# The feed-forward behind all blocks, in two halves of 1024 tokens, with seven quarter products in place of eight

## The chip, the cores and the metric

The kernel runs on one core of one Trainium2 chip. The metric is the time of one execution on the device, in microseconds (us); less is better. Inside the core five engines work side by side, each on its own instruction queue and in the order of that queue: TensorE (PE in the profile; its weight loads are PEld), VectorE (DVE), ScalarE (ACT), GpSimd (POOL) and SyncE (SP), which here issues all transfers (DMAs) between DRAM and the on-chip memory SBUF. TensorE adds its products up in the banks of PSUM, from where VectorE or ScalarE read them.

## What is computed

One layer of a hybrid decoder, for one prompt of 2048 tokens (width 1024) and for 64 sample rows (8 sequences of 8 tokens). Shapes and what doesn't matter here are left out:

```python
def hybrid_layer(x, c, ...):
    sh1, sc1, gt1, sh2, sc2, gt2 = split(silu(c) @ w_ada + b_ada, 6)
    h = rms_norm(x, norm1_g) * (1 + sc1) + sh1
    q, k, v, g, u, gate_r, gate_s = split(h @ w_in)
    ret = rms_normalize(retention(rotary(q), rotary(k), v)) * silu(g)
    ssm = gelu(s5(u)); ssm = ssm * sigmoid(ssm @ w_glu)
    merged = sigmoid(gate_r) * (ret @ w_br) + sigmoid(gate_s) * (ssm @ w_bs)
    x = x + gt1 * (merged @ w_out)
    h2 = rms_norm(x, norm2_g) * (1 + sc2) + sh2
    ff = square(relu(h2 @ w_up)) @ w_down        # 1024 -> 4096 -> 1024
    return x + gt2 * ff, ...
y = rms_norm(hybrid_layer(x, c, ...), norm_f_g)
```

The change concerns h2, ff and what follows. All is float32.

## The kernel before, in words

**Products.** A float32 operand is split in two parts: the high one (a copy rounded to the type fp32r, made by ScalarE) and the low one (the rest, a subtraction on GpSimd or VectorE). Each product is made as three matmuls, high by high, high by low and low by high, added up in PSUM. The unit is a matmul of a 128x128 stationary tile with 128x512 moving columns.

**Weights.** `plan` (L155) lays out one stream of weight tiles of 128x2x512 (512 KB). `fetch` (L162, its DMA on L165) loads a tile into one of four raw buffers, `refill` (L169) splits it: high half on L175, low half on L177, into a ring of five. One tile is fetched and split for each one used, so a load is issued as soon as the low half of an old tile is done.

**Blocks.** The tokens go through the layer in four blocks of 512; the sample's 64 rows ride along with block 1 (two more matmuls for each 128 rows of a weight, `sample_products`, L215). `super_block` (L1136) calls `block` (L191) for each group of 512 output columns, in the order u, q, k, v, g, gates, glu, br, bs, wo0, wo1, and then the feed-forward loop (L1434): up0, then for g from 1 to 7 up{g} followed by dn{g-1} in two halves a and b, and at the end dn7a with both halves. Each up group takes 96 matmuls and each dn half 48, so a block's feed-forward takes 16 x 96. What evacuates the banks: `ev_up` (L1385: ScalarE's relu, VectorE's product with the bank, ScalarE's and GpSimd's split of the result) and `ev_dn` (L1406: VectorE multiplies by gt2, L1411, and adds to the row tile x1, L1412). The activations and x1 stay in SBUF.

**Side work.** Everything that isn't a dense product (norms, retention, the S5 recurrence, outputs) is written as generators that `spawn` queues and `tick` advances a step after each piece of products. So the second norm (`norm_t`, L353 to L380: scale, eight transposes on TensorE at L365, eight modulations on VectorE at L377, split) is spawned by the evacuation of wo1 row tile by row tile, the first norm of the next block (`ln1`, L1094) at up7, and `output` (L1459: final norm, store) by dn7a. A scheduler then orders each engine's instructions; buffers come from pools, each name from a pool of fixed size, and a new tile waits until the readers of the buffer's old one are done. The pools that matter are `units` (15 buffers of 1 MB), `w2` (six tiles of up to 128x512) and `w4` (two of up to 128x1024); a tile that `work` gives comes from w2 or w4 by its size alone.

## Time and profile before

| what | value |
|---|---|
| times of three runs | 3221.25, 3223.88, 3227.47 us |
| median | 3223.88 us |
| span of the profiled execution | 3214.3 us |
| difference of the median to that span | 9.6 us |
| TensorE busy | 3066.6 us, 14460 matmuls |
| VectorE, GpSimd, ScalarE busy | 1782.5, 1527.6, 985.9 us |
| read from DRAM, written | 345.55 MB, 28.79 MB |

The span is the time from the first to the last instruction of one profiled execution. In rows of groups, `out<-in` are the kernel's tile names, then partitions x elements and type of both sides, `xN` the count, then busy time, mean time of one in ns, and the idle time of the engine just before them with what ended it. Rows of one tile or line give min/median/max in ns. Rows of the chain of waits give the start, the time it took in the chain, and what it was; rows of a timeline start, duration, engine, line; rows of stretches the length, then busy time (and count) of PE, PEld, DVE, ACT and POOL, the granted TensorE clock, the busy share of the DMA engines, and GB/s.

### The profile page before, as it was taken

How to read it: one execution, taken by the hardware profiler on the slowest of the kernel's cores; microseconds unless marked ns; L12 is line 12 of the kernel's file. 1: busy time of each engine (PE TensorE's matmuls, PEld its weight loads, DVE VectorE, ACT ScalarE, POOL GpSimd, SP SyncE). 2: the span in 40 equal slices, each digit the busy share in tenths (PEclk: the TensorE clock that was granted, in tenths of full speed). 3: DMA queues.
4: the chain of work that ended last, by engine and by line, in shares of the span. 5: the costliest groups of instructions: out<-in, count | busy, mean ns of one | idle time of the engine just before them, and what ended most of it. 6: DMA issues, size and time to landing. Idle time of an engine off the chain costs nothing.

```text
span 3214.3 us, 37740 instructions
## 1 busy us (share of the span) xinstructions
PE 3066.6 (95%) x14460; PEld 2524.0 (79%) x14460; DVE 1782.5 (55%) x3177; ACT 985.9 (31%) x1430; POOL 1527.6 (48%) x724
## 2 busy tenths in 40 slices
PE   7889999999899999899999899999998899999998
PEld 3667788888688887788887688888887788888886
DVE  5978445444867154645458673354547663354545
ACT  2323434222322232332324123332333223333332
POOL 2442465555343534354543334645563433646653
PEclk9989999999999999999999899999999999999999
DMA  8474542323464423132223642422323652333331
GB/s 221 154 237 144 165 138 79 100 97 98 117 185 119 115 71 118 59 99 79 80 85 100 185 150 74 126 98 98 98 95 103 189 152 81 119 100 97 98 99 66
DMA packets 233400, 376.80 MB, mean 117 GB/s; under 512 B 67766, under 2 KB 78534, under 8 KB 229115
## 3 DMA queue, kind: packets, MB, share of 16 engines
q1 hardware_dynamic: 233220, 374.40, 37.7%
q8 instruction: 113, 1.85, 0.2%
q14 instruction: 67, 0.55, 0.0%
HBM read 345.55 MB, written 28.79 MB: 116 GB/s over the span
## 4 chain that ended last, share of the span: by engine, by line
PE 75%; DVE 17%; DMA 3%; issue 2%; SPq 1%; POOL 0%; ACT 0%; DVEq 0%; ACTq 0%; POOLq 0%
PE pd_up L212 20%; PE pd_gs L212 5%; PE pd_gr L212 5%; PE pd_wo L212 5%; PE pd_br L212 3%; PE pd_g L212 2%; PE pd_bs L212 2%; DVE m L377 2%; PE pd_v L212 2%; PE pd_dn4a L212 1%; PE pd_dn3a L212 1%; PE pd_dn1a L212 1%; PE pd_dn5a L212 1%; PE pd_dn2a L212 1%; PE pd_dn0a L212 1%
## 5 line engine op out<-in xcount | busy, mean ns | idle before, releaser
L177 POOL TENSOR_TENSOR wlo<-wraw,whi 128x1024 fp32r<-128x1024 f32 x472 | 1189.6, 2525 | 1388.5 <-ACT whi L175 1169.7
L175 ACT ACTIVATE whi<-wraw 128x1024 fp32r<-128x1024 f32 x504 | 531.0, 1059 | 1403.5 <-PE pd_up L212 271.9
L212 PE MATMUL pd_up<-h2l,whi 128*128 128x512 f32 (+1 forms) x1152 | 422.8, 368 | 6.0 <-DVE h2l L380 3.3
L212 PE MATMUL pd_up<-h2h,whi 128*128 128x512 f32 (+1 forms) x1152 | 419.6, 368 | 8.6 <-ACT h2h L379 7.6
L212 PE MATMUL pd_up<-h2h,wlo 128*128 128x512 f32 (+1 forms) x1152 | 417.2, 367 | 0.0
L1389 DVE TENSOR_TENSOR tv<-tu,pd_up 128x512 f32<-128x512 f32 x128 | 87.8, 688 | 513.7 <-ACT tu L1388 513.0
L1412 DVE TENSOR_TENSOR x<-x,td 128x512 f32<-128x512 f32 x256 | 339.3, 1325 | 7.5
L212 PEld LDWEIGHTS pd_up<-h2h,whi 128*128 128x128 f32 x1152 | 217.2, 190 | 46.2 <-ACT h2h L379 9.3
L212 PEld LDWEIGHTS pd_up<-h2l,whi 128*128 128x128 f32 x1152 | 219.0, 190 | 43.0 <-DVE h2l L380 8.1
L212 PEld LDWEIGHTS pd_up<-h2h,wlo 128*128 128x128 f32 x1152 | 218.5, 190 | 34.9
L1391 POOL TENSOR_TENSOR al<-tv,ah 128x512 fp32r<-128x512 f32 x128 | 177.3, 1395 | 35.7 <-ACT ah L1390 32.8
L212 PE MATMUL pd_gr<-hh,whi 128*128 128x512 f32 x256 | 103.4, 405 | 2.3 <-DVE gU L1220 2.3
L212 PE MATMUL pd_gs<-hl,whi 128*128 128x512 f32 x256 | 101.0, 394 | 0.0
L212 PE MATMUL pd_gr<-hl,whi 128*128 128x512 f32 x256 | 101.0, 394 | 0.0
L212 PE MATMUL pd_gs<-hh,whi 128*128 128x512 f32 x256 | 100.7, 395 | 0.0
L212 PE MATMUL pd_wo<-whi,mh 128*128 128x512 f32 x256 | 100.3, 393 | 0.0
L212 PE MATMUL pd_wo<-wlo,mh 128*128 128x512 f32 x256 | 100.3, 393 | 0.0
L212 PE MATMUL pd_wo<-whi,ml 128*128 128x512 f32 x256 | 99.8, 394 | 0.0
L212 PE MATMUL pd_gs<-hh,wlo 128*128 128x512 f32 x256 | 99.4, 395 | 0.0
L212 PE MATMUL pd_gr<-hh,wlo 128*128 128x512 f32 x256 | 99.2, 393 | 0.0
L377 DVE TENSOR_SCALAR m<-pt,s,modT 128x128 f32<-128x128 f32 x256 | 85.6, 403 | 8.6 <-PE pt L365 6.8
L1388 ACT ACTIVATE tu<-pd_up 128x512 f32<-128x512 f32 x128 | 76.0, 595 | 45.0 <-PE pd_up L212 43.9
(674 smaller groups left out, 6897.9 us busy)
## 6 DMA issues: line engine op xcount, KB each, us to landing
wraw<-in_w_in_dram SPq DMA_DIRECT2D x144, 512.0 KB
wraw<-in_w_up_dram SPq DMA_DIRECT2D x128, 512.0 KB
wraw<-in_w_down_dram SPq DMA_DIRECT2D x128, 512.0 KB
s5p<-s5c SPq DMA_DIRECT2D x32, 1024.0 KB
wraw<-in_w_ada_dram SPq DMA_DIRECT2D x32, 512.0 KB
wraw<-in_w_out_dram SPq DMA_DIRECT2D x32, 512.0 KB
x<-in_x_prompt_dram SPq DMA_DIRECT2D x20, 512.0 KB
wa<-in_w_ada_dram SPq DMA_DIRECT2D x8, 1024.0 KB
```

The costliest lines, as they stand in the source:

```text
L175: a = nc.scalar.activation(hi, raw, AF.Copy)
L177: l = eng.tensor_sub(lo, raw, hi)
L212: nc.tensor.matmul(banks[j][:, cols], a, b, start=(k == 0 and z == 0), stop=(k == nk - 1 and z == 2))
L377: nc.vector.tensor_scalar(m[:, a], pt[:, a], s[:, k:k + 1], b[:, k:k + 1], op0=ALU.mult, op1=ALU.add)
L1388: nc.scalar.activation(t, p, AF.Relu)
L1389: V.tensor_mul(t2, t, p)
L1391: nc.gpsimd.tensor_sub(act[g][1][:, j], t2, act[g][0][:, j])
L1412: V.tensor_add(x[:, e], x[:, e], t)
```

## The change

The feed-forward leaves the blocks. A block ends with wo1. The row tile x1 is stored to DRAM (`x1d`), and `norm_quarters` replaces the second norm: the same scale, transposes and modulations, but the normed activations are written to DRAM (`s2d`) as seven "parts" of 128x2048 float32 (1 MB each; for blocks 1 and 3 the sums and differences with the parts of the block before, which are read back). Behind block 3, `feed_forward` runs two halves of 1024 tokens. Its products are made by Strassen's scheme in the variant of Winograd: the weight's and the activations' quarters are combined by sums and differences so that seven quarter products do the work of eight.

A half consists of five macros: one "up" of 16 quads (256 columns of w_up each) and four "down" (each 1024 rows of w_down) of four quads. A quad has seven products p in the order 1, 5, 6, 3, 7, 2, 4, each of four 128-rows x three matmuls: 84 matmuls, in four PSUM banks a (1, 6, 7), d (5, 3), b (2), c (4), which are read out after each product, also between products that add to one bank. For each quad two loads of 512 KB bring the weights (`quad_fetch`), and for each product `quad_split` makes the weight's quarter, for p = 5, 6, 7, 4 by a difference on GpSimd, and splits it (ScalarE; low half on VectorE for 7, 2, 4 and on GpSimd otherwise). At each macro's start all seven parts of the activations are loaded (`part_load`, two halves of 512 KB into w4 each) and split (`part_split`) into 14 tiles that the whole macro uses; the part for p is loaded within the last quad of the macro before, and a new part's split waits for the old part's last product. `evac_up` combines the up products with relu and square into seven parts again and stores them (`sd`, 2 DMAs a quad). `evac_down` adds each product, scaled by gt2, into an accumulator of 1024 tokens by 256 columns. After the last down macro's quads, `turn_back` transposes the accumulator (16 transposes a quad), adds x1 (loaded into w4), and after the fourth applies the final norm in place (32 instructions of 128x256, norm_f_g in w4) and stores (32 DMAs).

The sample's feed-forward becomes "side" tiles of the old stream, drawn one after each unit of the other products: its up in block 2, its down in block 3. `units` has 17 buffers in place of 15, the pool of small tiles 10 in place of 12, the block orders "h" and "jd" go, and the first norm of the next block is spawned before wo0. The pools of the blocks and those of the feed-forward take turns in the same memory. The core of the diff:

```diff
+ORDER = (1, 5, 6, 3, 7, 2, 4)
+BANK = {1: "a", 6: "a", 7: "a", 5: "d", 3: "d", 2: "b", 4: "c"}
...
+    def part_load(self, macro, p):
+        kind, k, c = macro
+        src = (self.s2d[k] if kind == "up" else self.sd[k][c])[PART[p]]
+        ts = []
+        for h in range(2):
+            t = self.work("sw", [P, 2, 512])
+            self.nc.sync.dma_start(t.rearrange("p a n -> p (a n)"), src[:, 1024 * h:1024 * h + 1024])
+            ts.append(t)
+        return ts
+
+    def part_split(self, p, ts):
+        hi = self.sring.tile([P, 4, 512], F32R, tag="s", name="shi")
+        lo = self.sring.tile([P, 4, 512], F32R, tag="s", name="slo")
+        for h, t in enumerate(ts):
+            a = slice(2 * h, 2 * h + 2)
+            self.nc.scalar.activation(hi[:, a], t, AF.Copy)
+            (self.nc.vector if (p + h) % 2 else self.nc.gpsimd).tensor_sub(lo[:, a], t, hi[:, a])
+        return hi, lo
...
+            elif p == 7:
+                copy(A21, b)
+                V.tensor_add(A22, A22, b)
+                relu2(A[:, 0:2].rearrange("p a n -> p (a n)"))
+            elif p == 2:
+                V.tensor_add(A11, A11, b)
+            else:
+                V.tensor_add(A21, A21, b)
+                relu2(A[:, 2:4].rearrange("p a n -> p (a n)"))
+                V.tensor_add(S[:, 0], A21, A22)
+                nc.gpsimd.tensor_sub(S[:, 2], A11, A21)
+                V.tensor_sub(S[:, 1], S[:, 0], A11)
+                V.tensor_sub(S[:, 3], A12, S[:, 1])
+                nc.sync.dma_start(dst[0:3, :, cols].rearrange("i p n -> p i n"), A[:, 0:3])
+                nc.sync.dma_start(dst[3:7, :, cols].rearrange("i p n -> p i n"), S)
...
+    def feed_forward(self):
+        es, pool = self.open(True)
+        self.sring, self.xring = pool("parts", 14), pool("stage", 4)
+        self.tring, self.traw = pool("tring", 8), pool("traw", 4)
+        macros = []
+        for k in range(2):
+            macros += [("up", k, 0)] + [("down", k, c) for c in range(4)]
...
+        for n, (macro, q) in enumerate(self.quads):
+            self.quad_fetch(n + 2)
+            last = n + 1 < len(self.quads) and self.quads[n + 1][0] != macro
...
+            for at, p in enumerate(ORDER):
...
+                if last:
+                    raw = self.part_load(self.quads[n + 1][0], p)
+                self.quad_products(banks[key], T[p], S[p], first)
+                evac(p, banks[key])
+                if n + 1 < len(self.quads):
+                    T2[p] = self.quad_split(n + 1, p)
+                if last:
+                    S2[p] = self.part_split(p, raw)
+                self.tick()
...
@@ def super_block
                 V.tensor_add(x[:, e], x[:, e], t)
                 if d:
-                    self.spawn(self.norm_t(x, self.s2[:, :, 0], self.modT[:, 24:32, 0], h2h, h2l, j), 1)
+                    nc.sync.dma_start(self.x1d[4 * b + j], x)
+                    self.spawn(self.norm_quarters(x, b, j), 20 + 5 * j if b < 3 else 1)
```

In the rows of the order that follow, a name's number tells its buffers apart, and the brackets name the engines and DMA queues that the instruction waits for. First SP, between the last wo1 and the first products of block 3's feed-forward, before:

```order
L165 DMA wraw_21002<-in_w_up_dram 128x2x512 [waits DMAHW5_49,DMAHW4_49,Pool_49]
L165 DMA wraw_21039<-in_w_up_dram 128x2x512 [waits DMAHW1_49,Pool_49]
L165 DMA wraw_21223<-in_w_up_dram 128x2x512 [waits DMAHW6_49,DMAHW2_49,Pool_49]
L165 DMA wraw_21242<-in_w_up_dram 128x2x512 [waits DMAHW7_49,DMAHW3_49,Pool_49]
L165 DMA wraw_21271<-in_w_up_dram 128x2x512 [waits DMAHW4_49,DMAHW0_49,Pool_49]
```

and now, where the feed-forward begins (nq and ab are tiles of `norm_quarters`, sw a half part):

```order
L654 DMA s2d_97<-nq_13800 512x1x128 [waits DMAHW5_49,Pool_49]
L659 DMA s2d_97<-ab_13801 512x1x128 [waits DMAHW6_49,Pool_49]
L656 DMA s2d_97<-nq_13831 512x1x128 [waits DMAHW7_49,DVE_49]
L358 DMA sw_13875<-s2d_96 128x1024 [waits DMAHW6_49,DMAHW0_49]
L654 DMA s2d_97<-nq_13831 512x1x128 [waits Pool_49]
L659 DMA s2d_97<-ab_13832 512x1x128 [waits DMAHW2_49,Pool_49]
L358 DMA sw_13877<-s2d_96 128x1024 [waits DMAHW3_49,DMAHW2_49]
L358 DMA sw_13888<-s2d_96 128x1024 [waits DMAHW4_49,DMAHW0_49,DVE_49]
L358 DMA sw_13890<-s2d_96 128x1024 [waits DMAHW5_49,DMAHW3_49,Pool_49]
```

Weight tiles alone stood there; now the loads of the first parts, which read what blocks 0 and 1 stored (s2d_96), stand behind the last row's stores to s2d_97. Second, TensorE where up passes to down, before (dn0a behind up1) and now (the first down quad behind the first half's 16 up quads; shi and slo are the halves of a part, tw a weight quarter):

```order
L212 MATMUL pd_dn0a_4348<-whi_4198,ah_3906 128x512 [waits DVE_49]
L212 MATMUL pd_dn0a_4348<-wlo_4199,ah_3906 128x512 [waits Pool_49]
L212 MATMUL pd_dn0a_4348<-whi_4198,al_3907 128x512
L212 MATMUL pd_dn0a_4348<-whi_4198,ah_3906 128x512 [waits Activation_49]
L212 MATMUL pd_dn0a_4348<-wlo_4199,ah_3906 128x512
L212 MATMUL pd_dn0a_4348<-whi_4198,al_3907 128x512 [waits Pool_49]
```

```order
L374 MATMUL pq_down_16273<-shi_16143,tw_16140 128x512 [waits Activation_49]
L374 MATMUL pq_down_16273<-slo_16144,tw_16140 128x512 [waits Pool_49]
L374 MATMUL pq_down_16273<-shi_16143,tw_16140 128x512 x2
L374 MATMUL pq_down_16273<-slo_16144,tw_16140 128x512
L374 MATMUL pq_down_16273<-shi_16143,tw_16140 128x512 x2
L374 MATMUL pq_down_16273<-slo_16144,tw_16140 128x512 [waits DVE_49]
L374 MATMUL pq_down_16273<-shi_16143,tw_16140 128x512 x2
L374 MATMUL pq_down_16273<-slo_16144,tw_16140 128x512
L374 MATMUL pq_down_16273<-shi_16143,tw_16140 128x512
L374 MATMUL pq_down_16290<-shi_16169,tw_16166 128x512 [waits Activation_49]
L374 MATMUL pq_down_16290<-slo_16170,tw_16166 128x512 [waits DVE_49]
```

Before, the operands of a product came from the weight ring and from activations in SBUF; now each product of the first quad of a macro waits for the split of its own part. Third, SP where the first half's last down passes to the second half's up; before, at a block's end, only weight tiles and the output stores of L1466 stood there:

```order
L358 DMA sw_18721<-s2d_97 128x1024 [waits DMAHW7_49,DMAHW1_49,Pool_49]
L358 DMA sw_18723<-s2d_97 128x1024 [waits DMAHW0_49,DVE_49]
L461 DMA xp_18772<-x1d_95 128x4x256 [waits DMAHW1_49,Pool_49]
L461 DMA xp_18774<-x1d_95 128x4x256 [waits DMAHW2_49,DVE_49]
L491 DMA nfg_18904<-in_norm_f_g_dram 128x1024 [waits DMAHW3_49,DVE_49]
L317 DMA traw_18957<-in_w_up_dram 128x4x256 [waits Pool_49]
L501 DMA out_0_dram<-acc_16272 8x16x256 [waits DVE_49]
L501 DMA out_0_dram<-acc_16402 8x16x256 [waits DVE_49]
```

The loads of x1 for the last quad's turning back (xp), those of norm_f_g (nfg) and the output stores follow the last of the 14 half loads of the new up, and the first two use the same two buffers.

More of the change, by code (lines that the diff above doesn't have):

```diff
@@ L92, in __init__, with open @@
         self.fillers = []
+    def open(self, tiles=False):
+        es = ExitStack()
+        pool = lambda name, bufs: es.enter_context(
+            self.tc.tile_pool(name=name, bufs=bufs, reuse_waits="tile" if tiles else "pool"))
+        return es, pool
     def unit(self, name, dt=F32, shape=(P, 4, 512)):
@@ L188, in weight, with refills, side @@
         return self.wq.pop(self.used - 1)
+    def refills(self):
+        while self.due:
+            self.due -= 1
+            self.refill()
+    def side(self):
+        if self.used >= len(self.stream) or self.stream[self.used][0][:2] not in SIDE:
+            return
+        name = self.stream[self.used][0]
+        src, evac = self.sides[name]
+        if name not in self.open_side:
+            self.open_side[name] = [self.bank(f"ps_{name}", [P, 512]), 0]
+        st = self.open_side[name]
+        nk = 32 if name[0] == "d" else 8
+        w = self.weight(name)
+        for kk in range(2):
+            for z in range(2):
+                k = st[1]
+                self.nc.tensor.matmul(st[0], src(k), w[z][:, kk], start=(k == 0 and z == 0),
+                                      stop=(k == nk - 1 and z == 1))
+            st[1] += 1
+        self.due += 1
+        if st[1] == nk:
+            del self.open_side[name]
+            self.spawn(evac(st[0]))
     def block(self, name, kind, src, evac=None, sample=None, order="k"):
@@ L281, in block @@
[L281 to L302 removed]
+        for j in range(4):
+            for u in range(nu):
+                for kk in range(2):
+                    products(2 * u + kk, j, ws[u], kk)
+                if u == nu - 1:
+                    evac(j, banks[j])
+                self.tick()
+                if j == 3 and not sample:
+                    self.refill()
@@ new lines, in evac_down, with put, f @@
+    def evac_down(self, macro, q):
+        nc, V = self.nc, self.nc.vector
+        c = macro[2]
+        if c == 0:
+            if q == 0:
+                self.acc = {}
+            self.acc[q] = self.xring.tile([P, 4, 512], F32, tag="x", name="acc")
+        acc = self.acc[q]
+        g = [self.modT[:, 40 + 2 * q + l, 0:1] for l in range(2)]
+        def put(i, l, b, new):
+            d = acc[:, 2 * i + l]
+            if new and c == 0:
+                nc.scalar.activation(d, b, AF.Copy, scale=g[l])
+            else:
+                V.scalar_tensor_tensor(d, b, g[l], d, op0=ALU.mult, op1=ALU.add)
+        def f(p, b):
+            if p == 1:
+                put(0, 0, b, True)
+            elif p == 5:
+                put(1, 1, b, True)
+            elif p == 6:
+                put(0, 1, b, True)
+            elif p == 3:
+                put(0, 1, b, False)
+            elif p == 7:
+                put(1, 0, b, True)
+                put(1, 1, b, False)
+            elif p == 2:
+                put(0, 0, b, False)
+            else:
+                put(1, 0, b, False)
+                if c == 3:
+                    self.spawn(self.turn_back(macro[1], q, self.acc), 2)
+        return f
@@ new lines, in super_block, with output_sample @@
+            self.sides |= {f"ds{d}": (lambda k: aS[k // 16][:, k // 4 % 4, k % 4], ev_ds(d)) for d in range(2)}
+        nxt = self.spawn(self.ln1(b + 1)) if b + 1 < NSB else None
+        self.block("wo0", "N", srcN(mh, ml), ev_wo(0), S(m2S, ev_woS(0)) if smp else None, order="j")
+        f = self.block("wo1", "N", srcN(mh, ml), ev_wo(1), S(m2S, ev_woS(1)) if smp else None, order="j")
+        self.finish(f, nxt)
+    def output_sample(self, x):
+        nc = self.nc
+        nfg = self.unit("nfg", shape=(64, D))
+        nc.sync.dma_start(nfg, raw_ap(self.i["norm_f_g"], 0, [[0, 64], [1, D]]))
```

458 lines of the change are left out of this document (266 added, 192 removed).

## The prediction

> **What bounds the kernel now.** I read the page first: the busy line, the DMA rate in 40 slices, and the share of the chain of waits by engine.
>
> ```profile
> span 3214.3 us, 37740 instructions
> PE 3066.6 (95%) x14460; PEld 2524.0 (79%) x14460; DVE 1782.5 (55%) x3177; ACT 985.9 (31%) x1430; POOL 1527.6 (48%) x724
> ...
> GB/s 221 154 237 144 165 138 79 100 97 98 117 185 119 115 71 118 59 99 79 80 85 100 185 150 74 126 98 98 98 95 103 189 152 81 119 100 97 98 99 66
> ...
> PE 75%; DVE 17%; DMA 3%; issue 2%; SPq 1%; POOL 0%; ACT 0%; DVEq 0%; ACTq 0%; POOLq 0%
> ```
>
> TensorE is busy for 95% of the span, so only fewer matmuls or fewer gaps can help, and what else leaves it idle costs in full. The profiled execution took 3214.3 us; the median of the three times is 3223.88, so I add 9.6 us to every span below. Next, the table by stretches: the four feed-forwards of before and the end.
>
> ```profile
> 498.80:873.60 374.80, 362.55 (x1688) 301.84 (x1689) 198.06 (x294) 121.53 (x175) 204.87 (x97) 0.99 0.32 101
> 1312.00:1755.20 443.20, 429.78 (x2008) 356.00 (x2007) 256.40 (x387) 142.08 (x214) 202.39 (x97) 0.99 0.26 84
> 2118.10:2490.10 372.00, 361.29 (x1681) 301.77 (x1682) 195.23 (x282) 120.68 (x170) 203.42 (x97) 0.99 0.31 99
> 2845.00:3201.20 356.20, 352.66 (x1648) 295.20 (x1648) 176.13 (x226) 108.63 (x148) 199.13 (x94) 1.00 0.28 90
> 3201.20:3214.30 13.10, 0.01 (x1) 0.00 (x0) 6.77 (x24) 0.72 (x2) 0.00 (x0) 0.60 0.39 120
> ```
>
> The four stretches last 1546.2 us. The chain of waits gives the price of a matmul and of a restart, and two DMA waits:
>
> ```profile
> 572.12 21.76 PE pd_up L212 x96
> 843.14 4.18 PE pd_dn7a L263 x9
> 1806.90 6.93 DMA wraw<-in_w_in_dram
> 2529.47 4.48 DMA wraw<-in_w_in_dram
> ```
>
> 21.76 / 96 = 0.2267 us a matmul of 128x512. The nine at 843.14, right after a wait, take 0.464 us each: TensorE restarts at half rate, and those nine lose 2.1 us.
>
> **What the change removes.** 4 blocks x 16 weight groups x 96 matmuls = 6144 become 64 quads x 84 = 5376. The 768 fewer give 768 x 0.2267 = **-174.1**. The sample's 256 matmuls move beside other blocks, same count, no gain. The feed-forward of before also has stalls: 1546.2 - 6400 x 0.2267 (the 256 of the sample with it) - 31 for 224 transposes at 0.137 (eight take 1.09 below) = 64.5 us, mostly around the norms at either end of each block's feed-forward. Those norms no longer stand between matmuls of one block: **-64.5**. What comes in their place is counted next. Gains together: -238.6.
>
> **The macro changes.** The quads come as ten macros (for each half one "up" of 16 quads, four "down" of 4). At each start all seven parts of the activations, 1 MB each, are loaded as 14 halves of 512 KB into the working pool w4, which has two buffers, and then split: ScalarE makes the high half, GpSimd or VectorE the low one. A buffer comes free when the low half is done, so each buffer has a cycle: load, high, low. The nearest rows are those of the weight tiles, which are as large as a half part: the groups by line, and the timeline of one load early in the program (its issue, and the first use that waited for it).
>
> ```profile
> L175 ACT ACTIVATE whi<-wraw 128x1024 fp32r<-128x1024 f32 x504 | 531.0, 1059 | 1403.5 <-PE pd_up L212 271.9 <-PE ps_up L219 99.6 <-issue 79.7
> L177 POOL TENSOR_TENSOR wlo<-wraw,whi 128x1024 fp32r<-128x1024 f32 x472 | 1189.6, 2525 | 1388.5 <-ACT whi L175 1169.7 <-issue 111.0 <-PE ps_wo L219 30.2
> L177 DVE TENSOR_TENSOR wlo<-wraw,whi 128x1024 fp32r<-128x1024 f32 x32 | 41.6, 1302 | 19.8 <-ACT whi L175 19.8
> 320.47 0.39 SPq L165 DMA_DIRECT2D wraw<-in_w_ada_dram  x1
> 324.17 1.06 ACT L175 ACTIVATE whi<-wraw 128x1024 fp32r<-128x1024 f32 x1 [1.50 <-DMA wraw<-in_w_ada_dram]
> L1391 POOL TENSOR_TENSOR al<-tv,ah 128x512 fp32r<-128x512 f32 x128 | 177.3, 1395 | 35.7 <-ACT ah L1390 32.8
> L1390 ACT ACTIVATE ah<-tv 128x512 fp32r<-128x512 f32 x128 | 79.4, 625 | 4.9 <-DVE tv L1389 4.9
> ```
>
> A load alone takes 324.17 - 320.47 = 3.70 us from issue to use; as a wait on the chain 4.48, and 6.93 at worst. I take 4.48, because two halves and the weights of the quads are always under way together. High 1.06, low (1.30 + 2.53) / 2 = 1.91; sum 7.45. Each of the two splits stands in an in-order queue behind the splits of the quad weights: half of a GpSimd operation of 1.395 and half of a ScalarE one of 0.625 are 1.0. The cycle is 8.4 us (from 6.6 with 3.70 and no queue, to 10.9 with 6.93).
>
> *Eight ordinary changes.* The first two halves are loaded ahead; they can be split only when the last quad's first product (2.7 us) has released the old part, and that takes 1.06 + 1.91. The six further turns end 2.7 + 3.0 + 6 x 8.4 = 56 to 58 us after the last quad's start (the low half on GpSimd or on VectorE). TensorE's order gives it 184 matmuls, 41.7 us, before the seventh part's second half, since products of the next quad are drawn ahead. Stall 16 each, **+128** (0 to 29 each over the cycle's bounds).
>
> *The first start.* The part loads stand on SP behind the stores of the last row of block 3, and so behind its whole norm. The end of the program of before shows most of that chain:
>
> ```profile
> 3200.82 0.39 PE L263 MATMUL pd_dn7a<-whi,al 128*128 128x512 f32 x1
> 3206.95 1.41 DVE L1465 SCALAR_TENSOR_TENSOR x<-x,y,nfg 128x512 f32<-128x512 f32 x2
> 840.23 1.09 PE L365 MATMUL pt<-cpk,xu 128*128 128x128 f32 x8 [1.61 <-DVE xu L358]
> L377 DVE TENSOR_SCALAR m<-pt,s,modT 128x128 f32<-128x128 f32 x256 | 85.6, 403 | 8.6 <-PE pt L365 6.8 <-PE pt L494 1.3
> ```
>
> From the last product's end, 3201.2, to the row's scale known, 3206.95, 5.75 us; transposes 1.09; eight modulations 8 x 0.403 = 3.2; the sum about 0.7: 10.8. A store about 5 (nearest row 4.48), a load 4.48, a split 3.7: 24. Then five turns of 8.4 (one half is on its way before the stores): 66. TensorE has 108 matmuls, 24.5 us, for that: **+42** (28 to 54).
>
> *The change to the second half's up.* SP's order has the last tile's two loads of x and norm_f_g in w4 too, behind all 14 half loads. Then VectorE adds, ScalarE squares, the Newton steps, 32 scalings and the output DMAs follow, and only they free the accumulator that the new up's first quad stages in.
>
> ```profile
> L1465 DVE SCALAR_TENSOR_TENSOR x<-x,y,nfg 128x512 f32<-128x512 f32 x32 | 26.8, 878 | 0.1
> L331 ACT ACTIVATE junk<-x 128x512 f32<-128x512 f32 x72 | 45.1, 626 | 127.1 <-DVE x L1355 49.8 <-DVE x L1412 41.1 <-DMA x<-in_x_prompt_dram 18.7
> L331 ACT ACTIVATION_READ_ACCUMULATOR junk<-x 128x1 f32 x72 | 13.4, 186 | 0.0
> L321 DVE SCALAR_TENSOR_TENSOR t<-y,v 128x1 f32<-128x1 f32 x144 | 53.5, 377 | 2.2
> L325 DVE SCALAR_TENSOR_TENSOR y<-t,y 128x1 f32<-128x1 f32 x144 | 49.6, 348 | 2.1
> ```
>
> A scaling of 128x256 is about half of the first row, 0.4, a square with its readout 0.31 + 0.19 and a gap, 0.54. With 56 for the 14 halves, one cycle for x (8.4), adds 4 x 1.3, squares 8 x 0.54 = 4.3, steps 2.4 (two of each kind and the start), 29 scalings 11.6, a store 3.7, this ends at 92 us; TensorE has 34 us until it needs the banks: **+58** (30 to 75).
>
> *Restarts.* Ten stops at 2.1: **+21**.
>
> **Steady quads.** A quad gives TensorE 84 x 0.2267 = 19.04 us. The others per up quad, from these and the rows above:
>
> ```profile
> L1412 DVE TENSOR_TENSOR x<-x,td 128x512 f32<-128x512 f32 x256 | 339.3, 1325 | 7.5
> L1389 DVE TENSOR_TENSOR tv<-tu,pd_up 128x512 f32<-128x512 f32 x128 | 87.8, 688 | 513.7 <-ACT tu L1388 513.0 <-POOL wlo L177 0.7
> L1412 DVE TENSOR_TENSOR x<-x,td x256: 673/693/2893, 553.9 to 3202.2; 128x512 f32<-128x512 f32 x128
> ```
>
> GpSimd nine operations (four differences, four low halves, one quarter) x 1.395 = 12.6; VectorE four adds with PSUM at 0.688 and ten pieces of 128x512 with SBUF alone (three low halves, three sums, two double-width squares), from 0.69 to 1.33: 10 to 16; ScalarE eleven x 0.62 = 6.8. All below 19.04, and each part of a bank has one product's time, 2.72 us, to be read before the next product adds to it. I charge 0.2 a quad for late reads: **+13** (0 to 96).
>
> By the Trainium skill, "GPSIMD Engine Reference" (the table of its interfaces), GpSimd shares VectorE's way into SBUF and gets in the way of VectorE instructions with two SBUF inputs. The rows agree: the sum of two SBUF tiles has a mean of 1325 ns and one as long as 2893, against 688 with an input in PSUM. Taken as a rule for the low halves and sums of this change, VectorE would stand nearer the upper end above, or beyond.
>
> **The rest.** The first norm of the next block ran under up and down matmuls; it is now drawn under wo, where VectorE has some 58 us of work (evacuation 8 x (0.688 + 1.325) and four rows of about 10.5: 8 x 0.403, six steps of 0.36, and 5 for scaling and low halves) in 48: with the restart, 9 at three borders, **+27** (0 to 50). Norms put off and the sample's tiles beside the blocks' products: **+10** (0 to 25). The end: evacuation and transposes 2.3, adds 5.2, squares 4.3, steps 2.4, 32 scalings 12.8, the last store 4.7, together 31.7 in place of the 13.1 in the table: **+19**. 96 more transposes x 0.137: **+13**. Adds together 42 + 128 + 58 + 21 + 13 + 27 + 10 + 19 + 13 = +331.
>
> Sum: 331 - 239 = +92, a span of 3306, a time of 3316 (+2.9%). One microsecond of the cycle is worth about 61 in all (eight ordinary changes x 6 turns, 5 at the start, 8 at the second up), so the change pays below a cycle of 6.9.
>
> **The rivals.** *The loads land early* (faster). With loads at 3.70 and hardly a queue, the cycle is 6.5: 1.9 x 61 = 116 less, and with shorter stalls half of the restarts (-11) and of the borders (-17) go: +92 - 144 = -52, a time of 3172. It decides below 6.9. For it: the unloaded row, 3.70, and the page's DMA row, whose slices reach 237 GB/s where loads are thickest. Against it: the chain's 4.48 and 6.93, at a mean rate lower than here. Chance 0.28.
>
> *VectorE becomes the bound of the steady quads.* With ten SBUF operations at 1.8 us (between 1.325 and the longest 2.89) and four at 0.688, an up quad takes VectorE 20.8: 32 x 1.8 = 57, and late reads of 0.8 in 32 down quads 26: 83 in place of 13, a time of about 3386. Chance 0.09.
>
> *TensorE stays at half rate through the changes.* In a change it works 2.7 us and waits for the next part, again and again. If the rate doesn't come back in between, the 24 matmuls after the last part take 0.237 more each, 5.7 us at ten places: about 3373. Against it, the nine matmuls at 843.14 were enough. Chance 0.12. The Trainium skill, "TensorE: Matmul & The Clock Gate" (Part 1), says that TensorE falls to half its clock after an idle window of about 3.4 us and needs a busy stretch to come back; that is this rival's rule, and the row's 4.18 us at half rate agrees.
>
> *It all but cancels*, within 0.2% (about what a measurement of this kernel can tell from no change): chance 0.03. My forecast keeps 0.48.
>
> **How the numbers follow.** Slower 0.48 + 0.09 + 0.12 = 0.69; faster 0.28; same 0.03. Low end 3180, just above the faster rival's centre, which leaves out half of it; the high end 3410 takes in both slow rivals and a cycle near 9.9. The slower cases' own range is 3250 to 3410.
>
> **What would show it.** In the profile after: about 13,790 matmuls on TensorE (14460 - 768 + 96); ten gaps in its busy row, each behind loads of the parts and ScalarE's or GpSimd's splits; a turn of a part buffer of about 8.4 us; at the second up a wait for the output's last scalings; steady quads at 19.0 to 19.3 us. I am wrong in the main if quads next to a macro change are as long as the others, or if quads far from one take over 20 us.

## The result, and the profile after

The changed kernel takes 3362.23 us (median of four, 3358.53 to 3365.42) against 3223.5 us before: a ratio of 1.042, 95% interval 1.040 to 1.044. That is slower, as forecast, and 46 us above the 3316 that the sum gave, inside the range of 3180 to 3410. The profiled execution has a span of 3363.3 us, 149.0 longer than that of before.

The page of the changed kernel, busy line and share of the chain of waits:

```profile
span 3363.3 us, 37072 instructions
PE 2984.7 (89%) x13436; PEld 2404.3 (71%) x13436; DVE 2090.4 (62%) x3229; ACT 1111.4 (33%) x1748; POOL 1835.9 (55%) x1002
...
PE 62%; DVE 15%; DMA 11%; POOL 5%; issue 3%; ACT 2%; SPq 1%; DVEq 0%; ACTq 0%; POOLq 0%
```

TensorE is busy 82 us less, so its work did go, but it now idles 11% of the span in place of 5%, and DMA and GpSimd have 16% of the chain where they had 3%. (13436 matmuls, not the 13,790 that the prediction expected to count: up0 of before was made in halves of 128x256, so that 384 products count twice there, and 32 of the 128 transposes of turning back were left out of the count.) Where the time went, by stretches of the changed kernel (length, then busy time and count of PE, PEld, DVE, ACT and POOL, granted clock, DMA share, GB/s):

```profile
0.00:1821.30 1821.30, 1668.45 (x7910) 1353.57 (x7911) 1140.01 (x2286) 589.38 (x871) 794.01 (x381) 0.95 0.52 156
1821.30:1869.60 48.30, 4.87 (x26) 3.83 (x24) 31.76 (x54) 5.86 (x10) 32.23 (x22) 0.55 0.71 206
1869.60:1919.80 50.20, 36.54 (x84) 22.95 (x85) 14.02 (x13) 19.16 (x23) 25.22 (x14) 0.65 0.46 147
1919.80:2186.40 266.60, 266.60 (x1177) 220.73 (x1177) 212.54 (x167) 87.64 (x154) 215.25 (x125) 1.00 0.46 155
2205.50:2249.30 43.80, 27.62 (x85) 18.61 (x85) 28.76 (x21) 17.06 (x23) 34.65 (x17) 0.81 0.62 210
2306.40:2339.90 33.50, 26.64 (x86) 18.35 (x85) 19.07 (x18) 13.02 (x16) 24.55 (x14) 0.80 0.58 188
2582.20:2661.40 79.20, 28.69 (x101) 21.11 (x100) 39.28 (x64) 20.05 (x37) 29.21 (x18) 0.66 0.47 153
3329.30:3363.30 34.00, 1.91 (x16) 1.46 (x14) 18.02 (x49) 3.30 (x16) 0.00 (x0) 0.58 0.41 139
```

The first row is the four blocks, the second the gap from wo1 to the first quad, the third that quad. The fourth is 14 up quads in a row: 266.6 / 14 = 19.04 us each, TensorE never idle. The next three are the quads at a change of macro, up to down, down to down, and down to the second half's up, each with 84 matmuls that take 19.04 us elsewhere: stalls of 24.8, 14.5 and 60.2 us. Cut up by 84 matmuls in TensorE's order, all 64 quads read like this: 54 take 19.0 to 19.3 or, where 16 transposes stand between them, up to 21.0; ten are long, and they are the first quad and those at the nine changes.

At a change, the chain of waits of the changed kernel shows the cycle that the sum was built on. From the third down macro of the first half, and from the second up:

```profile
2401.06 5.92 DMA sw<-sd
2406.98 0.02 issue
2407.00 1.07 ACT shi L367
2408.07 0.07 issue
2408.14 2.37 POOL slo L368
...
2422.79 4.23 DMA sw<-sd
2427.02 0.02 issue
2427.04 1.07 ACT shi L367
...
2616.61 1.07 ACT shi L367
...
2619.50 3.36 DMA xp<-x1d
...
2633.47 11.97 DVE acc L496 x30
...
2646.38 3.70 DMA out_dram<-acc
```

Load, high half, low half, and only then the next load. The last eight turns of a change, from one half load to the next into the same buffer, took 7.5 to 8.5 us on average, and 7.8 over all ten macros (forecast 8.4); single turns took 5.9 to 11.3. At the second up the loads of x1 do come behind the last part, then the 32 scalings, and ScalarE's first read-out of the new quad (`aq`) starts when the first output store has left the accumulator.

### The profile page after: what moved, and what is told of

It reads as the page before. It is cut to its first block, busy times and chain, and to the rows that moved or that the text cites. A ratio compares the mean times of both kernels' runs of the same rounds, so it can differ in the third digit from the quotient of the medians.

```text
span 3363.3 us, 37072 instructions
## 1 busy us (share of the span) xinstructions
PE 2984.7 (89%) x13436; PEld 2404.3 (71%) x13436; DVE 2090.4 (62%) x3229; ACT 1111.4 (33%) x1748; POOL 1835.9 (55%) x1002
## 4 chain that ended last, share of the span: by engine, by line
PE 62%; DVE 15%; DMA 11%; POOL 5%; issue 3%; ACT 2%; SPq 1%; DVEq 0%; ACTq 0%; POOLq 0%
PE pq_up L374 16%; PE pq_down L374 11%; PE pd_gr L252 5%; PE pd_gs L252 5%; DMA sw<-sd 4%; PE pd_br L252 3%; PE pd_wo L252 3%; PE pd_bs L252 2%; POOL slo L368 2%; DMA xu<-in_x_prompt_dram 2%; PE pd_k L252 2%; PE pd_g L252 2%; PE pd_u L252 2%; DMA sw<-s2d 1%; PE pd_glu L252 1%
## 5 line engine op out<-in xcount | busy, mean ns | idle before, releaser
L193 POOL TENSOR_TENSOR wlo<-wraw,whi 128x1024 fp32r<-128x1024 f32 x248 | 615.9, 2495 | 791.1 <-ACT whi L190 658.3
L374 PE MATMUL pq_down<-shi,tw 128*128 128x512 f32 x1792 | 587.8, 406 | 60.5 <-ACT shi L367 31.0
L374 PE MATMUL pq_up<-shi,tw 128*128 128x512 f32 x1792 | 569.2, 398 | 78.8 <-ACT shi L367 49.8
L190 ACT ACTIVATE whi<-wraw 128x1024 fp32r<-128x1024 f32 x312 | 323.7, 1056 | 634.0 <-issue 64.5
L374 PEld LDWEIGHTS pq_down<-shi,tw 128*128 128x128 f32 x1792 | 348.6, 195 | 151.8 <-ACT shi L367 47.5
L374 PEld LDWEIGHTS pq_up<-shi,tw 128*128 128x128 f32 x1792 | 344.6, 192 | 157.1 <-ACT shi L367 55.5
L374 PE MATMUL pq_down<-slo,tw 128*128 128x512 f32 x896 | 364.2, 407 | 25.5 <-POOL slo L368 14.8
L374 PE MATMUL pq_up<-slo,tw 128*128 128x512 f32 x896 | 357.7, 399 | 7.1 <-POOL slo L368 4.8
L349 POOL TENSOR_TENSOR tw<-ts,tw 128x512 fp32r<-128x512 f32 x128 | 229.9, 1810 | 42.1 <-ACT tw L348 37.7
L330 POOL TENSOR_TENSOR ts<-traw 128x512 f32<-128x512 f32 x128 | 200.3, 1565 | 41.7 <-DVE tw L349 35.9
```

Source lines behind the costliest of these rows:

```text
L190: a = nc.scalar.activation(hi, raw, AF.Copy)
L193: l = eng.tensor_sub(lo, raw, hi)
L330: G.tensor_sub(t, a, b)
L349: (V if p in (7, 2, 4) else G).tensor_sub(t[:, 1], x, t[:, 0])
L374: self.nc.tensor.matmul(bank, w, x, start=(first and a == 0 and z == 0), stop=(a == 3 and z == 2), skip_group_check=True)
```

## The experiments

Each expectation stands as it was written before the run. Every run but the last is a single one. Stalls are the length of a quad's 84 matmuls less 19.04; "the changes" are the eight ordinary ones together.

### The parts without the two buffers

```diff
 def part_load:
-            t = self.work("sw", [P, 2, 512])
-            self.nc.sync.dma_start(t..., src[...])
+        lo = self.sring.tile([P, 4, 512], F32R, tag="s", name="slo")
+        raw = lo.bitcast(F32)
...
+            self.nc.sync.dma_start(raw[:, 2 * h:2 * h + 2]..., src[...])
 def part_split:
+            t = raw[:, a]
             self.nc.scalar.activation(hi[:, a], t, AF.Copy)
             (...).tensor_sub(lo[:, a], t, hi[:, a])
 feed_forward:
+                self.quad_products(banks[key], T[p], S[p], first)
                 if last:
                     raw = self.part_load(self.quads[n + 1][0], p)
-                self.quad_products(banks[key], T[p], S[p], first)
```

The last lines belong to the edit: a part's load now needs the tile of an old part, so it is drawn behind that part's last product and no longer ahead of it.

> The parts are loaded straight into the tiles that hold their low halves and are split there in place, so that up to seven parts are under way and w4's two buffers no longer stand between them; the arithmetic and all loads stay. Theory (the two buffers' cycle of 7.4 to 8.5 us makes the stalls): the eight ordinary changes, 138 us of stalls now, fall to under 25 in all; the second up, 60, falls to 30 to 45, since x1 and norm_f_g no longer queue behind the 14 half loads, but the 32 scalings stay; the feed-forward's start, 48 + 31, loses some 20. Together a time of about 3190. Rival (the in-order queues of GpSimd and ScalarE set the rate of the splits): the changes keep 10 us and more each, the time stays above 3290.

3279.76 us, 82 less than the changed kernel. The eight ordinary changes fell from 138 to 90, not below 25; the second up from 60 to 43, the first quad's stall from 31 to 14, while the gap ahead of it grew from 48 to 52. So taking the two buffers away is worth a third of the eight changes' stalls, and something else holds the rest at 8 to 18 each. The subtractions of the low halves in the changed kernel, then in this one, and one stop of TensorE in its timeline, show what (min/median/max in ns):

```profile
L368 DVE TENSOR_TENSOR slo<-sw,shi x70: 1218/1316/2311, 1869.6 to 3267.1; 128x1024 fp32r<-128x1024 f32 x70
L368 POOL TENSOR_TENSOR slo<-sw,shi x70: 2338/2384/3387, 1875.6 to 3263.7; 128x1024 fp32r<-128x1024 f32 x70
```

```profile
L369 DVE TENSOR_TENSOR slo<-slo,shi x70: 1216/2296/3437, 1867.5 to 3174.3; 128x1024 fp32r<-128x1024 f32 x70
L369 POOL TENSOR_TENSOR slo<-slo,shi x70: 2337/2848/3415, 1868.8 to 3174.5; 128x1024 fp32r<-128x1024 f32 x70
```

```profile
2286.84 3.37 DVE L369 TENSOR_TENSOR slo<-slo,shi 128x1024 fp32r<-128x1024 f32 x1
...
2290.13 1.40 DVE L430 SCALAR_TENSOR_TENSOR acc<-pq_down,modT,acc 128x512 f32<-128x512 f32 x2
2291.01 0.77 PE L375 MATMUL pq_down<-shi,tw 128*128 128x512 f32 x1 [5.08 <-DVE acc L430]
```

A low half that VectorE can do in 1.22 us took it 2.3 in the median and up to 3.4; the read-out of a PSUM bank (L430) stood behind one of 3.37, and TensorE waited 5.08 us for that bank. With several parts arriving at once, GpSimd and VectorE do their subtractions at the same time: of VectorE's 70, 64 overlapped work of GpSimd, in the changed kernel 55.

### GpSimd out of the feed-forward

The same edit was made to the changed kernel, whose parts still go through w4, and to a stack of the edits of this chapter (`e5_stack`: e3_late_norm and e4_early_x, below):

```diff
-            G.tensor_sub(t, a, b)
+            V.tensor_sub(t, a, b)
-        (V if p in (7, 2, 4) else G).tensor_sub(t[:, 1], x, t[:, 0])
+        V.tensor_sub(t[:, 1], x, t[:, 0])
-            (self.nc.vector if (p + h) % 2 else self.nc.gpsimd).tensor_sub(lo[:, a], t, hi[:, a])
+            self.nc.vector.tensor_sub(lo[:, a], t, hi[:, a])
-                nc.gpsimd.tensor_sub(S[:, 2], A11, A21)
+                V.tensor_sub(S[:, 2], A11, A21)
```

> The changed kernel with one edit, that of e6_no_gpsimd: no subtraction on GpSimd in the feed-forward; the part loads still go through w4's two buffers. Two-buffer theory: the cycle is 4.5 + 1.06 + 1.25 + queue, about 7.0 in place of 7.4 to 8.5, so the eight changes fall from 138 to about 90 to 110 and no further. Blocking theory (GpSimd against VectorE is the larger cause): they fall below 60. Rival (VectorE full): they grow.

3313.13 us. The changes fell to 98, at 6.6 to 7.8 us a turn (7.1 over all ten macros): the two-buffer theory's number, not the blocking theory's.

> As e5_stack, and in the feed-forward no subtraction runs on GpSimd: the weight differences, all low halves and the one quarter go to VectorE. Theory (what is left at the changes after e1_inplace, 8 to 18 us each, is GpSimd and VectorE blocking each other: a low half of 128x512 took VectorE 0.68 to 2.9 us): VectorE's means fall to 0.7 for 128x512 and 1.25 for 128x1024, VectorE has about 16 of 19 us in an up quad and no quad gets longer, the eight changes fall from 90 to under 50 us, the time by 30 to 70. Rival (VectorE is simply full without GpSimd's share): up quads go over 19.5 and changes stay or grow, the time rises by 20 or more.

3149.35 us against 3219.16 of e5_stack: 70 us less. Here the changes, 98 in e5_stack, fell to 50. The tile of the weight quarters and that of the parts, after (e6_no_gpsimd):

```profile
L349 DVE TENSOR_TENSOR tw<-ts,tw x256: 675/683/1187, 1788.5 to 3090.9; 128x512 fp32r<-128x512 f32 x128
...
L349 DVE TENSOR_TENSOR tw<-traw,tw x192: 672/683/694, 1786.1 to 3087.6; 128x512 fp32r<-128x512 f32 x192
```

```profile
L369 DVE TENSOR_TENSOR slo<-slo,shi x140: 1206/1216/1227, 1796.4 to 3042.2; 128x1024 fp32r<-128x1024 f32 x140
```

In the changed kernel the like rows were 678/1189/2884 for VectorE and 1263/2027/2283 for GpSimd:

```profile
L349 DVE TENSOR_TENSOR tw<-ts,tw x128: 678/1189/2884, 1840.5 to 3308.1; 128x512 fp32r<-128x512 f32 x128
L349 POOL TENSOR_TENSOR tw<-ts,tw x128: 1263/2027/2283, 1834.7 to 3294.7; 128x512 fp32r<-128x512 f32 x128
```

VectorE alone does GpSimd's share too in 56.2 of 76 us of steady up quads (stretch 2600 to 2676), where the two engines together had been busy 80% each. Taken together: two things stood in a row at the changes. With the buffers in place, relief of the engines gives what a shorter cycle gives (138 to 98); without the buffers, 86 to 98 are left (e1_inplace to e5_stack), and with GpSimd out as well 50. That step holds two gains which no run separates: the engines no longer slow each other, and the low halves that GpSimd made, 2.34 us at least, take VectorE 1.22.

### The second up, and the end

```diff
-        for t in range(8):
-            for n in range(4):
+        for n in range(4):
+            for t in range(8):
                 V.scalar_tensor_tensor(o[:, t], o[:, t], r[:, t:t + 1], nfg[...], ...)
+                nc.sync.dma_start(..., o[:, t])
```

> As e1_inplace, and turn_back scales and stores the output column group by column group (all 8 row tiles of one accumulator first), so that the first accumulator is free after 8 of 32 scalings. Theory: the second up then waits for the first accumulator only, its stall falls by 15 to 25 us against e1_inplace, and the end of the program changes by less than 5. Rival (the chain ahead of the scalings, loads of x1, adds, squares and Newton steps, fills the stall): less than 5 us in all.

3264.10, 15.7 less than e1_inplace. The second up fell from 43 to 35, less than forecast: the chain ahead of the scalings (adds, squares, Newton steps at 1.2 us each beside the others' work) is the larger part now. Of the rest of the 15.7, 5.5 lie in the blocks, whose code is the same (see below on scatter). The end didn't change, 34 us; a row of its timeline:

```profile
3236.05 22.11 SPq L499 DMA_DIRECT2D out_dram<-acc  x32
```

32 stores of 128 KB take SP 22.1 us from the first to the last. Was that the issuing, or the transfers? Two runs:

```diff
+        for t in range(8):                       # gain applied group by group, before r is known
+            V.tensor_mul(rows[:, t], rows[:, t], nfg)
...
+                if t % 8 in (1, 4, 6):
+                    nc.scalar.activation(o[:, t], o[:, t], AF.Copy, scale=r[:, t:t + 1])
+                else:
+                    V.tensor_scalar(o[:, t], o[:, t], r[:, t:t + 1], None, op0=ALU.mult)
+                (nc.scalar if k and t % 2 else nc.sync).dma_start(..., o[:, t])
```

> As e6_no_gpsimd, and the end of each half is rebuilt: the gain norm_f_g is multiplied in group by group before the row scale is known, the last scaling is a product with the row scale alone, shared by VectorE and ScalarE, and in the second half every second store is issued by ScalarE. Theory (in e2_by_column the end is 34 us: 12.8 of scalings and 22 of SP issuing 32 stores at 0.69): the end falls to 20 to 25, the second up by 3 to 8, the time by 12 to 22. Rival (the landing of the stores sets the end): under 5.

3149.36, the same as e6_no_gpsimd; the end 34.1. The second up, which was to fall by 3 to 8, rose from 26 to 32. VectorE's scalings were done in 5.3 us in place of 12.8, and two queues issued. The rival held: a stretch of that end, and the chain of waits, show the stores running with nothing else going on.

```profile
3130.00:3134.00 4.00, 0.00 (x0) 0.00 (x0) 0.00 (x0) 0.00 (x0) 0.00 (x0) 0.50 0.54 192
```

```profile
3129.66 5.03 DMA out_dram<-acc
...
3134.76 4.97 DMA out_dram<-acc
```

4 MB at 192 GB/s are 21.8 us, and the DMA engines' share stood at 0.54.

```diff
-            for t in range(8):
-                nc.sync.dma_start(raw_ap(..., [[D, 8], [8 * D, 16], [1, 256]]), o[:, t])
+            for a in range(8):
+                nc.sync.dma_start(raw_ap(..., [[8 * D, 16], [P * D, 8], [1, 256]]), o[16 * a:16 * a + 16])
```

> As e6_no_gpsimd, and the output of a half is stored in 32 pieces cut along the other axis: each store takes 16 partitions with all 8 row tiles of a column group (its outermost count is 16 where it was 8); bytes and number of stores stay. Theory (in e7_end the end was set by the stores, 4 MB at 192 GB/s with the DMA engines' share at 0.54, because a transfer with 8 as its outermost count keeps only half of the engines busy): the share goes to 0.8 and more, the end falls from 34.5 by 5 to 10 us; the scalings of 12.8 and the issues remain. Rival (192 GB/s is what 1 KB pieces get, or SP's issue sets it): the end stays within 3.

3135.82, but the end took 35.0. The share went up as forecast, and the rate did not:

```profile
3115.00:3120.00 5.00, 0.00 (x0) 0.00 (x0) 3.86 (x10) 0.00 (x0) 0.00 (x0) 0.50 0.91 195
3120.00:3125.00 5.00, 0.00 (x0) 0.00 (x0) 0.00 (x0) 0.00 (x0) 0.00 (x0) 0.50 0.88 200
```

So the theory was right on the engines and wrong on the time, by either half of the rival. Which half is open, since all stores were issued by SP again:

```profile
3109.39 21.07 SPq L500 DMA_DIRECT2D out_dram<-acc  x32
```

128 KB every 0.66 us are 199 GB/s, so the issuing alone allows no more than was measured. In e7_end two queues issued, but with the outermost count of 8; no run has both two queues and 16, so what pieces of 1 KB can get isn't shown. The Trainium skill, "DMA: Bandwidth & Descriptors" (Rules for kernel authors), says that an outermost count below 16 confines a transfer to that many engines; the shares of 0.54 and 0.9 agree. The 13.5 us by which this run lies under e6_no_gpsimd are in the blocks (10.3) and the changes, not at the end.

### The start of the feed-forward

```diff
 ev_wo:
-                    self.spawn(self.norm_quarters(x, b, j), 20 + 5 * j if b < 3 else 1)
+                    if b < 3:
+                        self.spawn(self.norm_quarters(x, b, j), 20 + 5 * j)
 feed_forward:
+        for j in range(4):          # block 3's rows: read back from x1d, normed beside the up quads
+            self.spawn(self.norm_quarters(None, 3, j), 8 + 16 * j)
...
```

> As e2_by_column, and block 3's second norm no longer runs before the feed-forward: its four rows are read back from x1d and normed beside the first half's up quads (one row in 16 ticks). Theory (the start's 79 us are the serial chain norm, store, read back, store, first part): the start loses 35 to 60 us against e2_by_column, steady up quads stay at 19.0 to 19.4. Rival (VectorE is too full beside the up quads): the first dozen up quads go over 20 us each and give 10 us and more back.

3259.71, only 4.4 less than e2_by_column, and yet both theories were right: the gap from wo1 to the first quad fell from 52 to 9 us, and the up quads beside the late rows gave 21 back (two of them 7.5 and 8.4, where the row's transposes held TensorE's queue and waited 3.8 and 4.9 us for VectorE to scale the row); the blocks came out 11 longer. With the rows 30 ticks apart (e5_stack) the up quads lost 5.

### The borders between blocks, and a stack

```diff
+        x1 = [...]; self.x_rows(x1..., b, j); gt1 = ...; self.mod_row(gt1, 2)
         for d in range(2):
             self.block(f"br{d}", ...)
...
         for d in range(2):
             self.block(f"bs{d}", ...)
-        x1 = [...]; self.x_rows(x1..., b, j); gt1 = ...; self.mod_row(gt1, 2)
```

> The changed kernel with one edit: the loads of x1 and gt1 are issued ahead of br0 in place of after bs1, so that they no longer run together with the four loads of x for the next block's first norm. Theory (the three borders wo to u lose 17 to 22 us each to eight row loads at once, at about 130 GB/s): wo falls from 67 to 48 to 52 us in blocks 0 and 2, the time by 35 to 55, to about 3315. Rival (VectorE has 58 us of work in 48, as forecast): wo stays above 60, the time within 10 us.

3334.92, 27 less. The wo groups of blocks 0, 1 and 2, by stretches, in the changed kernel and then in e4_early_x:

```profile
457.30:523.90 66.60, 53.15 (x234) 43.49 (x232) 42.44 (x104) 21.15 (x39) 23.44 (x12) 0.87 0.47 121
919.00:992.80 73.80, 59.39 (x254) 47.65 (x254) 46.98 (x106) 19.22 (x36) 18.41 (x9) 0.88 0.41 133
1365.50:1433.40 67.90, 53.41 (x226) 43.49 (x225) 40.11 (x93) 19.47 (x34) 22.65 (x12) 0.85 0.47 120
```

```profile
461.80:510.40 48.60, 48.44 (x234) 39.77 (x232) 40.14 (x104) 21.39 (x39) 23.73 (x12) 1.00 0.41 115
908.40:972.60 64.20, 55.15 (x254) 45.21 (x254) 46.80 (x106) 18.92 (x36) 18.44 (x9) 0.95 0.34 112
1347.00:1394.70 47.70, 47.54 (x226) 39.34 (x225) 37.74 (x92) 19.73 (x34) 22.84 (x12) 1.00 0.39 117
```

48 us less at the three, with VectorE as busy as before: the amount of VectorE's work was not the cause. In the changed kernel's timeline and chain at block 2's wo:

```profile
1385.55 0.69 DVE L1636 SCALAR_TENSOR_TENSOR tw<-pd_wo,gt 128x512 f32<-128x512 f32 x1 [15.65 <-DMA gt<-modd]
```

```profile
1370.25 27.44 DMA xu<-in_x_prompt_dram
```

VectorE stood 15.65 us idle for the load of gt1, and the loads of x for the next block's norm had 27.44 us of the chain. Of the 48, the time kept 27 against the median and 30.5 against the profiled execution: the blocks ended 42 us earlier, and 11 went back in the feed-forward, nearly all of it at the changes (138 to 149), whose code is the same.

> e3_late_norm and e4_early_x together, the four late rows 30 ticks apart in place of 16. If the two gains are of different places they add: 3259.7 - 27 to 30, and 5 to 15 more from the spread rows (quads 1 to 7 lost 21 us in e3_late_norm): 3210 to 3228. If the early loads only move the wait into the next block, under 15 in all: 3245 and more.

3219.16, 40.6 less than e3_late_norm, as forecast, but not made up as forecast: the blocks ended 40.5 us earlier, and the feed-forward as a whole lost only 0.9. The spread rows gave back 16 in the up quads, while the first quad's stall rose by 7 and the changes by 8. This is the first version whose single run is no slower than the kernel before.

```diff
 x_rows:
-        src = raw_ap(self.i["x_prompt"], ..., [[D, 8], [8 * D, 16], [1, D]])
-        return self.nc.sync.dma_start(t, src)
+        for a in range(8):
+            self.nc.sync.dma_start(t[16 * a:16 * a + 16], raw_ap(..., [[8 * D, 16], [1, D]]))
```

> As e6_no_gpsimd, and each load of a 128-row tile of x is issued as eight loads of 16 partitions. Theory as in e9_stores_by_16, for loads: the four loads of x for the next block's norm take less time together, wo of block 1 falls from 70 to 62 or less and blocks 0 and 2 by 0 to 3. Rival (SP's queue, with 8 times as many issues for x at about 0.4, delays the weights): wo stays or grows and the time rises by 5 to 30.

3141.24, 8 less than e6_no_gpsimd, which is within the scatter below. wo of block 1 fell from 70 to 64, but it lies between 64 and 71 in the other kernels with the early x1. Those of blocks 0 and 2, which were to fall by 0 to 3, rose by 4.7 and 2.6. No gain is shown.

### The price of the eighth product

```diff
                 self.quad_products(banks[key], T[p], S[p], first)
+                if p == 4:
+                    self.quad_products(banks[key], T[p], S[p], False)
```

> As e6_no_gpsimd with eight products a quad: product 4 is made twice (so its term is counted double in the output; the run is for its time alone). It gives the price of the product saved, in this order of the work: TensorE does 64 x 12 x 0.2267 = 174 us more, longer quads hide 10 to 30 of what stalls now at the changes, so the time rises by 145 to 165, to about 3305. If the splits and the loads were the limit beside TensorE, it would rise by less than 120.

3295.35, 146 more than e6_no_gpsimd. The feed-forward, first to last product, took 1476.9 in place of 1317.3, 159.6 more, and the blocks, with the same code, 13.5 less. So in this version the product saved is worth its matmuls, less some 14 us that longer quads hide, and with eight products it is slower than the kernel before (3229 us) by 66 us: the new order of the work costs that much even here.

### The best version, timed

> The kernel of e9_stores_by_16 once more, now timed in rounds against the kernel before. By the single looks of it and of e6_no_gpsimd and e7_end, which differ from it only in the end (3136 to 3149), 3130 to 3150 against 3223 to 3229: a ratio of 0.970 to 0.977. If the looks were chance, within 1% of the kernel before.

It has all edits but those of e7_end and e10_x_by_16: parts split in place, no GpSimd in the feed-forward, late norm of block 3, early x1, scaling by column group, stores by 16. 3140.52 us (3134.11 to 3144.19, six runs) against 3229.16 of the kernel before: a ratio of 0.972, interval 0.970 to 0.975. Its page:

```profile
PE 2918.5 (93%) x13436; PEld 2379.8 (76%) x13436; DVE 2179.6 (69%) x3843; ACT 1107.7 (35%) x1748; POOL 821.3 (26%) x388
```

A caution on the single runs: the blocks of e6_no_gpsimd, e7_end, e9_stores_by_16, e10_x_by_16 and e11_eight_products have the same code up to the feed-forward but for x's loads, and ended between 1771 and 1785 us. The eight changes differ by 7 to 11 us between kernels with the same code there (138 and 149, 43 to 50). Differences under some 15 us between two of these kernels are read from the stretch that was edited, not from the time.

## Why the prediction was right, point by point

The rows above against the terms of the sum, in us:

| term | forecast | measured |
|---|---|---|
| 768 matmuls fewer | -174.1 | steady quads at 19.04; 159.6 of 174 by e11_eight_products, in another version |
| stalls of the old feed-forward | -64.5 | -71.5 by the count below, not tested apart |
| eight ordinary changes, with their restarts | 128 + 17 | 138 |
| second up, with its restart | 58 + 2 | 60.2 |
| start, with its restart | 42 + 2 | 48.3 + 31.2 = 79.5 |
| steady quads | 13 | about 0 |
| borders wo to u | 27 | 52 |
| norms put off, side tiles | 10 | 35 |
| end | 19 | 34.0 - 13.1 = 21 |
| more transposes | 13 | 11 |
| old transposes that moved into the start | none | -3 |
| sum | +92 | +149 |

The prediction took 224 transposes off the old feed-forward's stretches, but 50 of them stood in the wo groups; with 174, its stalls were 71.5. The two measured block terms (borders, norms put off) come from the first stretch: 1821.3 - 1655.0 of before, less 58.0 for the sample's 256 matmuls and 20.8 for 152 transposes that moved in (22 more moved into the start), leaves 87.5; the three wo groups took 60.9 more than those of before, in the rows

```profile
453.30:498.80 45.50, 45.49 (x209) 37.52 (x207) 27.33 (x57) 15.47 (x26) 22.52 (x12) 1.00 0.45 132
1255.60:1312.00 56.40, 50.88 (x218) 41.27 (x218) 22.41 (x42) 11.03 (x21) 17.94 (x9) 0.94 0.40 118
2072.60:2118.10 45.50, 45.46 (x209) 37.48 (x207) 25.98 (x57) 15.50 (x26) 22.74 (x12) 1.00 0.48 135
```

of which 8.5 are 62 more transposes (96 of the next block's norm, where 34 of the second norm stood before); 52.4 are the borders, and 35.1 the rest. Since the table divides up the two spans, its sum agrees with their difference by construction; the single rows are what tests the forecast.

**Right, for the reasons given.** The direction; the steady quads; the changes as the largest cost; their cycle of load, high half and low half; the second up with its chain in the order forecast (14.0 us from the last part's split to the first scaling in place of 20.3, scalings of 12.0 for 11.6, a store of 3.7). The step from cycle to stall holds change by change: in the trace of the changed kernel, the seventh part's second half is split 52.5 to 56.4 us after the last quad's start at the six changes from down to down (forecast 56 to 58), and 65 us at the two from up to down. Less the 41.7 us of matmuls, that gives 11 to 15 and 23 to 24; the measured stalls are 12.5 to 20.2 and 24 to 25. That the eight together came so near the forecast is in part luck: the turns were shorter than forecast, and the two changes from up to down longer.

**Right in size by luck.** The end, 34.0 us for 31.7. The sum had 14.2 us ahead of the scalings, and the changed kernel's timeline shows 7.3, since the squares run beside the adds. It had one store of 4.7 behind the scalings, but the 32 stores were on SP's queue for 21.7 us almost from the first scaling on, 9 us past the last one. The two errors all but cancel.

**Right in size, half right in cause.** The changes were put down to two buffers. e8_vector_staged, e1_inplace and e6_no_gpsimd together show two causes in a row: the buffers, and behind them the splits on GpSimd and VectorE, which slow each other and stand in VectorE's queue ahead of the read-out of PSUM. Taking away one leaves 90 to 98 of 138. The sum had only the 1.0 us for "half of an operation" ahead in a queue for the second cause. The prediction did say that GpSimd gets in VectorE's way, but priced it for the steady quads alone, where TensorE never waited for it.

**Wrong in mechanism.** The borders. The step that failed is "VectorE has some 58 us of work ... in 48". VectorE was busy 40 to 47 us and idle while it waited for gt1 and x; e4_early_x took 48 us off without touching its work. (The step's own arithmetic was off as well: 58 in 48 with a restart of 2.1 is 12 a border, not 9.) The prediction noted that the next norm was drawn under wo, but counted only its VectorE instructions and not its four row loads, which fall together with the four of x1 on the same queue.

**Mis-sized.** The start. The sum priced one row's norm ahead of the stores, 24 us to the first part. The chain of waits of the changed kernel in the gap:

```profile
1823.21 2.55 DVE nq L643 x8
...
1853.97 4.41 DMA s2d<-ab
1858.39 3.27 DMA ab<-s2d
...
1864.94 5.04 DMA s2d<-ab
1870.00 4.47 DMA sw<-s2d
```

VectorE still had the modulations of three rows to do; then each row reads back what block 2 stored, in a buffer of w4, and waits for the store of the row before; and the parts' second buffer of w4 was held by the last `ab` until its store of 5.04 had landed. With 48.3 in place of 24 to the first product, and 31.2 in it, the term should have been 80. The norms put off and the sample's tiles come to 35 in place of 10. That is a remainder, and its cause stays open: single Newton steps of 128x1 took up to 2.4 us in the blocks, but they did so in the kernel before too.

**The rivals.** Faster needed a cycle of 6.5; it was 7.5 to 8.5 on average at each change. VectorE as the bound of the steady quads didn't come: it was busy 212.5 of 266.6 us. TensorE at half rate through the changes is partly true: in the quad from 2306.4 to 2339.9 its 86 matmuls were busy 26.64 us where 19.5 is full rate, so 7 us were slow matmuls, not 2.1. The granted clock there was 0.5 for 13.7 us, though TensorE was never idle for more than 2.2 us at a stretch, less than the window that the prediction names. But little of it was on the path: behind the last wait of over 0.9 us in each of the eight ordinary changes, 12 to 17 matmuls lost 0.1 to 2.6 us, 5.8 in all, where the rival had 5.7 at each place.

## What to carry to other kernels

A step that reloads all of an engine's operands at once is paid at its seams: count the seams, and price each as the longer of the loads' cycle (buffers, load, split) and the queue of every engine that the splits share with the read-out, because taking one away uncovers the other. A rearrangement that saves products can lose for reasons that have nothing to do with products: here the same seven products gave +4.2% as written and -2.8% with the edits of f_best: the parts split where they land, the feed-forward's subtractions on one engine, the loads of x1 and gt1 and a norm moved, the output scaled and stored in another order. Whether the kernel before would gain from the like, of its subtractions on GpSimd above all, no run tells. When work is moved to another place in the program, list its loads there too, with what is already on that queue.

## What the runs showed of the hardware

Two engines were slower together than one alone. In the changed kernel's feed-forward, VectorE's 128x512 subtractions of two SBUF tiles (`tw`) took 0.68 to 0.69 us where they overlapped no work of GpSimd (43 of them), and 1.77 in the median, up to 2.88, where they did (149). GpSimd's took 1.26 to 1.31 us alone (55), and 1.73 in the median, up to 2.29, beside VectorE's work (200). All of it on VectorE ran faster than shared: the feed-forward fell from 1392 to 1317 us between e5_stack and e6_no_gpsimd. The Trainium skill, "SBUF — State Buffer" (SBUF: two separate sides), calls the shared access an exclusive lock. The medians agree: a wait for up to one whole operation of the other engine would make 1.94 of 0.68 and 1.26; VectorE's longest, 2.88, is more than one such wait.

Stores in pieces of 1 KB ran at 192 GB/s with the DMA engines' share at 0.54 and two queues issuing, and at 195 to 200 with the share at 0.9 and one queue issuing 128 KB every 0.66 us.
